# Neighbourhood projections as 512-wide products on four PSUM banks, five gates written beside the first attention, last key factors on the vector engine

## The chip, the cores and the metric

One core of a Trainium2 chip. The metric is the device time of one launch in microseconds (us); three executions of the kernel before took 1293.41, 1294.27 and 1298.26 us, so its median is 1294.27 us.

## What is computed

Two layers over 256 context and 256 latent tokens of width 1024, all in float32. Cut to what matters:

```
for l in range(2):
    mod = silu(c) @ w_ada[l] + b_ada[l]               # six rows of 1024: shift, scale, gate, twice
    p = modulate(rms_norm(x), sh1, sc1) @ w_in[l]     # one projection, by columns:
    gate_logits, c_q, c_kv, k_r, na = split(p)        # 2048 | 768 | 256 | 32 | 3 x 512
    mq = rms_norm(c_q) @ w_uq                         # 8 heads of 96
    k_nope, mv = rms_norm(c_kv) @ w_ukv               # 8 heads of 64 + 64
    mq, mk = rms_norm(mq), rms_norm(cat(k_nope, k_r)) # rotary part turned for latent tokens
    y_mla = softmax(mq mk') mv                        # the first attention
    nq, nk = rms_norm(na[0]), rms_norm(na[1]); nv = na[2]
    y_na = softmax(nq nk' + bias in a window, context keys) nv   # the second attention
    y = sigmoid(gate_a) * (y_mla @ w_mla_o) + sigmoid(gate_b) * (y_na @ w_na_o)
    x = x + gt1 * (y @ w_out)
    x = x + gt2 * (relu(modulate(rms_norm(x), sh2, sc2) @ w_ff1)^2 @ w_ff2)
```

Layer 1 is the last: queries, gates and all behind them are made there for the 256 latent tokens alone. Its modulation is computed during layer 0.

## The kernel before, in words

**Products.** Every projection is three TensorE products per block (`mm3`, lines 100 to 103): high by high, high by low, low by high. A weight tile of 1024 columns per partition comes from DRAM into one of 5 `raw` tiles (line 106); `wsplit` (lines 127 to 132) makes its high part on ScalarE (L130) and its low part on VectorE (L131) into one of 3 `whi`/`wlo` pairs. `proj_a` (lines 134 to 151) keeps the weights stationary; `proj_b` (line 561) keeps the tokens stationary and streams the weights, for two token blocks of 128 at a time.

**Order of the work.** A planner places the instructions: each engine takes the ready instruction that was written first, in a modelled clock, and the resulting order of each engine is fixed when the kernel runs. What is written later fills the time in which what is written earlier waits. Tiles of one name are handed out in the order in which they are written. The order around the change, within a layer, is:

1. query products with `w_uq` (lines 721 to 730): three column chunks of 288, 288 and 192; then `w_ukv` (lines 733 to 746), two chunks of 512;
2. statistics (`q_stat`, `k_stat`), key factors (`k_fin`, line 748) and the rotary part (`q_fin`, line 706), all on GpSimd (POOL);
3. `gates(NG0[l], "B")` (line 760): 6 of the 16 gate column blocks in layer 0, 8 in layer 1, in PSUM tiles `psB`. A gate is one weight tile and 24 products, 512 wide in layer 0 and 256 in layer 1; its tanh (L679) goes to DRAM. Then `step(99)` (line 761), the rest of the running modulation;
4. the first attention (`attend_mla`);
5. the neighbourhood projections (`chunk_na`, line 964): parts 1 (keys), 0 (queries), 2 (values), each as two halves of 256 columns, both token blocks of a pair in one `psA` tile; each half holds two weight tiles until its last token block is done;
6. the second attention (`attend_na`), whose bias additions (L816) are queued on POOL behind the last `q_fin` (line 815);
7. `gates(16 - ngate[0])` (line 1010): the other 10 gates of layer 0, 8 of layer 1, in `psA`; then `step(99)` (line 1011);
8. the merge: products with `w_mla_o` and `w_na_o`, and so on.

**Modulation beside it.** `ada_side` (line 236) is a generator that computes modulation rows on VectorE in steps; `step(n)` advances it by n. A row takes 8 steps of one weight tile each (two VectorE products of 128x1024, L251 for the first tile, L255 for the others; each queued on VectorE behind the latest `wlo` then written), two steps that transpose and sum the accumulators (L266, L267, through `tmp` tiles, which a gate's tanh uses too) and one that ends it with a product on TensorE (L273) and the bias (L277). In layer 0 row 2 runs up to the first attention. Rows 4 and 3, scale and shift of the second norm, follow from line 991 on; both use one accumulator tile named `v`, of which there is one, so row 3 starts when the sums of row 4 are done. Of their 22 steps 6 are taken in the neighbourhood projections and one per gate in item 7; `step(99)` writes what is left.

Of the kernel before, what the change touches and what calls it, by code (L numbers as in the profile page):

```python
# [14 lines left out]
KD = 8  # L15
# [30 lines left out]
def trunk(ctx: ExitStack, tc, t):  # L46
# [10 lines left out]
    def ps(tag):  # L57
        return pp.tile([128, 512], F32, tag="ps" + tag, name="ps" + tag, bufs=BANKS[tag])
# [406 lines left out]
    for l in range(DEPTH):  # L465
# [92 lines left out]

        turn = [0]

        def proj_b(load, nk, act_h, act_l, toks, N, evac, banks=None):

            tiles = [load(i) for i in range(nk)]
            total = sum(len(x[2]) for x in tiles)
            for p0 in range(0, len(toks), 2):
                pair = toks[p0:p0 + 2]
                if banks == "one":
                    o = ps("A")
                    outs = [o[:, i * N:(i + 1) * N] for i in range(2)]
                else:  # L570
                    turn[0] += 1
                    outs = [ps(b)[:, :N] for b in (banks[p0 // 2] if banks else ("AA", "BB")[turn[0] % 2])]
                parts = [list(zip(outs, pair))] if banks != "one" else [[x] for x in zip(outs, pair)]
                for part in parts:
                    n = 0
                    for wh, wl, ks in tiles:
                        for j, k in enumerate(ks):
                            for o, tk in part:
                                cs = slice(tk * 128, (tk + 1) * 128)
                                mm3(o, act_h(k)[:, cs], act_l(k)[:, cs], wh[:, j], wl[:, j], n == 0, n == total - 1)  # L580
                            n += 1
                for o, tk in zip(outs, pair):
                    evac(tk, o)

# [129 lines left out]
        def k_stat(t):  # L714
            z = krr[:, t:t + 2, :]
            nc.gpsimd.tensor_tensor(out=z, in0=z, in1=krs[:, t:t + 2].unsqueeze(2).to_broadcast([128, 2, NH]), op=ALU.add)
            fin_r(z.rearrange("p t h -> p (t h)"), z.rearrange("p t h -> p (t h)"), QK)
            nc.gpsimd.tensor_tensor(out=krz[:, t:t + 2, :], in0=z,
                                    in1=rk[:, t:t + 2].unsqueeze(2).to_broadcast([128, 2, NH]), op=ALU.mult)

        for h0, n in ((0, 3), (3, 3), (6, 2)):
            def evac(tk, o):
                dst = mq[:, tk, h0:h0 + n, :]
                nc.scalar.activation(out=dst, in_=o.rearrange("p (h d) -> p h d", h=n), func=AF.Copy)
                head_ss(qrs[:, tk, h0:h0 + n], dst, n, QK, rq[:, tk - q0:tk - q0 + 1])
                if h0 == 6 and tk % 2:
                    q_stat(tk - 1)

            proj_b(loader(t["w_uq"][l], 0, h0 * QK, n * QK, 3, 2), 2, lambda k: ch[:, k], lambda k: cl[:, k],
                   list(range(q0, 4)), n * QK, evac)  # L730


        for hf in range(2):
            def evac(tk, o):
                hs = slice(hf * 4, (hf + 1) * 4)
                src = o.rearrange("p (h d) -> p h d", h=4)
                rs = rk[:, tk:tk + 1]
                dst = mk[:, tk, hs, 0:NOPE]
                nc.vector.tensor_copy(dst, src[:, :, 0:NOPE])
                nc.scalar.activation(out=mv[:, tk, hs, :], in_=src[:, :, NOPE:128], func=AF.Copy, scale=rs)  # L740
                head_ss(krr[:, tk, hs], dst, 4, NOPE, rs)
                if hf == 1 and tk % 2:
                    k_stat(tk - 1)

            proj_b(loader(t["w_ukv"][l], 0, hf * 512, 512, 2, 1), 1, lambda k: ch[:, 6 + k], lambda k: cl[:, 6 + k],
                   [0, 1, 2, 3], 512, evac)

        def k_fin(tk):
            z = mk[:, tk, :, 0:NOPE]
            nc.gpsimd.tensor_tensor(out=z, in0=z, in1=krz[:, tk, :].unsqueeze(2).to_broadcast([128, NH, NOPE]),  # L750
                                    op=ALU.mult)
            nc.gpsimd.tensor_tensor(out=mk[:, tk, :, NOPE:QK], in0=kr[:, tk, :].unsqueeze(1).to_broadcast([128, NH, RD]),
                                    in1=krr[:, tk, :].unsqueeze(2).to_broadcast([128, NH, RD]), op=ALU.mult)

        for tk in range(4):
            k_fin(tk)
        for tk in range(q0, 4):
            q_end = q_fin(tk)

        gates(NG0[l], "B")  # L760
        step(99)


# [31 lines left out]
        def prep_na(hp):  # L795
# [165 lines left out]

        nrs = ap.tile([128, 8, NH], F32, name="nrs")

        def chunk_na(part, half, toks):
            def evac(tk, o):
                cs = slice(half * 256, (half + 1) * 256)
                if part == 2:
                    nc.scalar.activation(out=nv[:, tk, cs], in_=o, func=AF.Copy)
                    return
                i = 4 * part + tk  # L970
                nc.scalar.activation(out=nqk[:, i, cs], in_=o, func=AF.Copy)
                head_ss(nrs[:, i, half * 4:half * 4 + 4], nqk[:, i, cs].rearrange("p (h d) -> p h d", h=4), 4, HD)
                if half == 1:
                    fin_r(nrs[:, i, :], nrs[:, i, :], HD)
                    z = nqk[:, i, :].rearrange("p (h d) -> p h d", h=NH)
                    nc.gpsimd.tensor_tensor(out=z, in0=z, in1=nrs[:, i, :].unsqueeze(2).to_broadcast([128, NH, HD]),
                                            op=ALU.mult)

            proj_b(loader(w_in, 0, OFF_NA + part * 512 + half * 256, 256, 4, 8), 2, H, Lo, toks, 256, evac, "one")
# [341 lines left out]
```

## Time and profile before

| | |
|---|---|
| median of three executions | 1294.27 us |
| the profiled execution, its own time | 1295.01 us |
| its span, first to last instruction | 1293.2 us |
| TensorE (PE) busy | 1267.5 us, 98% |
| VectorE (DVE) busy | 913.5 us, 71% |
| ScalarE (ACT), GpSimd (POOL) busy | 582.5 and 264.2 us |
| mean granted TensorE clock | 0.997 of full speed |

A matmul's row lasts from its start to its modelled end and overlaps the next; how fast TensorE works is read from the distance between two starts. The busy share of an engine is the union of its rows, so a PE that is busy may still wait for less than a row's length between two products.

### The profile page before, as it was taken

Reading aid. Unit: us, or ns where it says so; the run is one execution under the profiler, and the core shown is the slowest. Engines: PE = TensorE matmul, PEld = TensorE weight load, DVE = VectorE, ACT = ScalarE, POOL = GpSimd, SP = SyncE. Lnnn points to the kernel's source line nnn. Section 1 sums busy time; section 2 is a strip of 40 time slices with the busy share of each in tenths; the row PEclk is TensorE's granted clock in tenths of the full one; section 3 lists DMA queues with packets and bytes.
Section 4 is the critical chain, followed back from the end, with each engine's and each line's share of the span. In section 5 each row is a group of like instructions: output and inputs, shape, how many; then the busy total and the mean of one; then the engine's idle time right before and its main releaser. Section 6 shows DMA issues by size and latency. Waiting matters only on the chain.

```text
span 1293.2 us, 20347 instructions
## 1 busy us (share of the span) xinstructions
PE 1267.5 (98%) x7831; PEld 1090.8 (84%) x7831; DVE 913.5 (71%) x1547; ACT 582.5 (45%) x1054; POOL 264.2 (20%) x258
## 2 busy tenths in 40 slices
PE   7999999999999999999999999999999999999997
PEld 5698878986788898888788888998889789999896
DVE  4557987588985579898897844766763977665553
ACT  4455376445523343422322312466664555555452
POOL 0317501411005003210210200019122112211011
PEclk9999999999999999999999999999999999999999
DMA  8854710364497316565598732487214658646652
GB/s 280 298 122 139 236 34 17 104 191 65 100 316 227 96 58 201 164 200 182 166 293 271 211 98 87 132 175 213 67 44 116 134 184 223 175 161 189 190 192 84
DMA packets 241730, 208.01 MB, mean 161 GB/s; under 512 B 24337, under 2 KB 220689, under 8 KB 241249
## 3 DMA queue, kind: packets, MB, share of 16 engines
q1 hardware_dynamic: 236112, 199.59, 53.1%
q10 hardware_dynamic: 5008, 6.85, 1.5%
q8 instruction: 61, 1.00, 0.3%
q0 software_dynamic: 512, 0.27, 0.1%
q14 instruction: 37, 0.30, 0.1%
HBM read 195.15 MB, written 11.53 MB: 160 GB/s over the span
## 4 chain that ended last, share of the span: by engine, by line
PE 52%; DVE 3%; DMA 2%; issue 2%; ACT 2%; POOL 2%; SPq 0%; POOLq 0%; ACTq 0%; DVEq 0%
PE psA L101 6%; PE psA L103 6%; PE psA L102 6%; PE psB L101 6%; PE psB L102 6%; PE psB L103 6%; PE psC L103 4%; PE psC L101 4%; PE psC L102 4%; ACT whi L130 1%; PE psC L871 1%; DVE wlo L131 1%; PE psD L891 1%; DMA raw<-in_w_out_dram 1%; DMA raw<-in_w_ukv_dram 1%
## 5 line engine op out<-in xcount | busy, mean ns | idle before, releaser
L131 DVE TENSOR_TENSOR wlo<-raw,whi 128x1024 fp32r<-128x1024 f32 (+3 forms) x252 | 312.3, 1240 | 174.6 <-ACT whi L130 171.3
L130 ACT ACTIVATE whi<-raw 128x1024 fp32r<-128x1024 f32 (+3 forms) x252 | 261.0, 1036 | 357.9 <-PE psB L102 104.3
L255 DVE SCALAR_TENSOR_TENSOR ada<-raw,silu,ada 128x1024 f32<-128x1024 f32 (+1 forms) x126 | 160.6, 1309 | 0.5
L101 PE MATMUL psA<-whi,h 128*128 128x256 f32 (+2 forms) x408 | 120.4, 295 | 0.5 <-ACT h L345 0.4
L103 PE MATMUL psA<-whi,h 128*128 128x256 f32 (+2 forms) x408 | 120.4, 295 | 0.0
L102 PE MATMUL psA<-wlo,h 128*128 128x256 f32 (+2 forms) x408 | 120.3, 295 | 0.0
L102 PE MATMUL psB<-h,whi 128*128 128x256 f32 (+1 forms) x272 | 91.9, 338 | 0.9 <-DVE h L1045 0.9
L101 PE MATMUL psB<-h,whi 128*128 128x256 f32 (+1 forms) x272 | 91.8, 338 | 0.0
L103 PE MATMUL psB<-h,wlo 128*128 128x256 f32 (+1 forms) x272 | 91.7, 337 | 0.0
L101 PE MATMUL psA<-h,whi 128*128 128x512 f32 (+1 forms) x248 | 87.7, 354 | 1.0 <-ACT h L345 0.8
L102 PE MATMUL psA<-h,whi 128*128 128x512 f32 (+1 forms) x248 | 87.4, 352 | 0.2 <-DVE h L347 0.2
L103 PE MATMUL psA<-h,wlo 128*128 128x512 f32 (+1 forms) x248 | 87.2, 352 | 0.0
L101 PEld LDWEIGHTS psA<-whi,h 128*128 128x128 f32 x408 | 77.9, 191 | 2.8 <-ACT h L345 0.9
L102 PEld LDWEIGHTS psA<-wlo,h 128*128 128x128 f32 x408 | 77.8, 191 | 2.5 <-issue 0.8
L103 PEld LDWEIGHTS psA<-whi,h 128*128 128x128 f32 x408 | 77.8, 191 | 1.9
L1174 POOL TENSOR_TENSOR h<-s,h 128x512 fp32r<-128x512 f32 (+1 forms) x32 | 38.7, 1210 | 170.7 <-ACT h L1173 153.3
L1174 POOL TENSOR_TENSOR fl<-s,fa 128x512 fp32r<-128x512 f32 (+1 forms) x32 | 35.1, 1098 | 163.9 <-ACT fa L1173 163.9
L101 PE MATMUL psB<-G,whi 128*128 128x512 f32 (+2 forms) x192 | 66.7, 347 | 0.0
L103 PE MATMUL psB<-G,wlo 128*128 128x512 f32 (+2 forms) x192 | 66.2, 345 | 0.3 <-DVE wlo L131 0.3
L102 PE MATMUL psB<-G,whi 128*128 128x512 f32 (+2 forms) x192 | 66.4, 346 | 0.0
L101 PE MATMUL psC<-G,whi 128*128 128x258 f32 (+2 forms) x200 | 62.7, 314 | 0.0
L102 PE MATMUL psC<-G,whi 128*128 128x258 f32 (+2 forms) x200 | 62.5, 312 | 0.0
(388 smaller groups left out, 3333.1 us busy)
## 6 DMA issues: line engine op xcount, KB each, us to landing
raw<-in_w_ff_dram SPq DMA_DIRECT2D x128, 512.0 KB, 4.1
raw<-in_w_ada_dram SPq DMA_DIRECT2D x80, 512.0 KB, 4.5
raw<-in_w_in_dram SPq DMA_DIRECT2D x62, 512.0 KB, 4.4
raw<-in_w_out_dram SPq DMA_DIRECT2D x16, 512.0 KB, 7.0
spare<-in_w_ada_dram SPq DMA_DIRECT2D x12, 512.0 KB, 8.9
xT_d<-xT SPq DMA_DIRECT2D x2, 2048.0 KB, 13.0
bias<-in_rpb_dram SPq DMA_DIRECT2D x64, 64.0 KB, 7.3
g_d<-g ACTq DMA_DIRECT2D x16, 256.0 KB, 4.5
```

The costliest lines, as they stand in the source:

```text
L101: nc.tensor.matmul(out, sh, mh, start=first, stop=False)
L102: nc.tensor.matmul(out, sh, ml, start=False, stop=False)
L103: nc.tensor.matmul(out, sl, mh, start=False, stop=last)
L130: first = nc.scalar.activation(out=hi, in_=src, func=AF.Copy).ins
L131: split[:] = [nc.vector.tensor_tensor(out=lo, in0=src, in1=hi.bitcast(F32), op=ALU.subtract).ins, first]
L255: nc.vector.scalar_tensor_tensor(out=a, in0=raw[:, c:c + w], scalar=sc, in1=a, op0=ALU.mult, op1=ALU.add)
L871: nc.tensor.transpose(o[:, kt * 256 + i * 128:kt * 256 + (i + 1) * 128], pt[:, (kp * 2 + kt) * 128:(kp * 2 + kt + 1) * 128], perm if K == ...
L891: mm = nc.tensor.matmul(yo[z * 64:(z + 1) * 64, oc], vsel(kt, 2 * hp + z), tr[kt // 2][:, kt % 2, :], start=kt == nkt - 1, stop=kt == 0, t ...
L1174: nc.gpsimd.tensor_tensor(out=al[:, f, :], in0=s[:, :TQ], in1=ah[:, f, :].bitcast(F32), op=ALU.subtract)
```

## The change

It does four things. The neighbourhood projections are 512 wide: a part is one product of 512 columns for all its token blocks at once, in four PSUM banks (two `psA`, and two `psB` or one `psD` and one `psB`), one weight tile after the other; in layer 1 the order of the parts is 0, 1, 2. The query product has two chunks of 512 and 256 columns and a modulation step behind each. The gates are 5 before the first attention, 5 written behind it and ahead of the start of rows 4 and 3, so that no step goes with these, and the other 6 beside the second attention, in both layers. In layer 1 `k_fin` of the two latent token blocks runs on VectorE; and the bias additions are queued on POOL behind the last `k_stat` rather than the last `q_fin`. The steps beside the projections are two behind part 0 and one per weight tile of part 2.

```diff
-NG0 = (6, 8)
+NG = ((5, 5), (5, 5))
...
-        for h0, n in ((0, 3), (3, 3), (6, 2)):
+        for c0, n, h0, nh, kper in ((0, 512, 0, 5, 2), (512, 256, 5, 3, 3)):
             def evac(tk, o):
...
+            proj_b(loader(t["w_uq"][l], 0, c0, n, kper, 6 // kper), 6 // kper, lambda k: ch[:, k], lambda k: cl[:, k],
+                   list(range(q0, 4)), n, evac)
+            step()
...
         def k_fin(tk):
             z = mk[:, tk, :, 0:NOPE]
+            eng = nc.vector if last and tk >= 2 else nc.gpsimd
...
-        gates(NG0[l], "B")
+        gates(NG[l][0], "B")
         step(99)
...
-                with tc.issue_after(q_end.ins):
+                with tc.issue_after(k_end[-1]):
...
-        def chunk_na(part, half, toks):
+        def chunk_na(part, toks, banks):
+
+            outs = [ps(b) for b in banks[:len(toks)]]
+            load = loader(w_in, 0, OFF_NA + part * 512, 512, 2, 4)
+            for i in range(4):
+                wh, wl, ks = load(i)
+                for j, k in enumerate(ks):
+                    for o, tk in zip(outs, toks):
+                        cs = slice(tk * 128, (tk + 1) * 128)
+                        mm3(o, hh[:, k, cs], hl[:, k, cs], wh[:, j], wl[:, j], k == 0, k == KD - 1)
+                if part == 2:
+                    step()
...
-            if (part, half) in ((0, 1), (2, 0), (2, 1)):
+            if part == 0:
                 step(2)
 
+        gates(NG[l][1])
         if l == 0:
             av = []
...
-        for part in (1, 0, 2):
-            for half in range(2):
-                chunk_na(part, half, list(range(q0, 4)) if part == 0 else [0, 1, 2, 3])
+
+        for part, banks in ((0, "AA"), (1, "AABB"), (2, "AADB")) if last else ((1, "AABB"), (0, "AABB"), (2, "AADB")):
+            chunk_na(part, list(range(q0, 4)) if part == 0 else [0, 1, 2, 3], banks)
```

## Rows read from the trace of the kernel before

**Rows 1.** The page: busy time of the engines.
```profile
PE 1267.5 (98%) x7831; PEld 1090.8 (84%) x7831; DVE 913.5 (71%) x1547; ACT 582.5 (45%) x1054; POOL 264.2 (20%) x258
```

**Rows 2.** Busy time by stretch. First the stretch in us, then its length, then busy us (instructions) of PE, PEld, DVE, ACT and POOL, the granted clock, the DMA share and GB/s. Layer 0: projections alone, second attention, the gates that are left; layer 1: projections alone, second attention.
```profile
234.00:276.00 42.00, 42.00 (x351) 42.00 (x352) 26.55 (x29) 16.70 (x32) 14.96 (x12) 1.00 0.51 154
276.00:352.00 76.00, 75.05 (x455) 51.81 (x454) 69.56 (x160) 43.16 (x105) 6.37 (x5) 1.00 0.47 96
352.00:376.00 24.00, 24.00 (x106) 19.84 (x107) 23.05 (x23) 6.89 (x9) 0.00 (x0) 1.00 0.83 261
...
964.00:1000.00 36.00, 36.00 (x303) 36.00 (x302) 11.42 (x15) 15.14 (x29) 12.53 (x13) 1.00 0.42 118
1000.00:1051.00 51.00, 50.63 (x375) 39.70 (x373) 47.05 (x96) 30.95 (x68) 5.56 (x4) 1.00 0.55 122
```

**Rows 3.** The timeline of PE at four places where nothing waits: start in us, length, engine, line, operation. Two pairs of starts in the query product (288 columns, five products from the first to the second; 192 columns, six), one in layer 0's gates up to the merge (512 columns, three) and one in layer 1's (256 columns, fifteen).
```profile
91.03 0.29 PE L101 MATMUL psB<-whi,G 128*128 128x288 f32 x1
...
91.69 0.30 PE L103 MATMUL psB<-whi,G 128*128 128x288 f32 x1
...
104.03 0.27 PE L101 MATMUL psA<-whi,G 128*128 128x192 f32 x1
...
104.70 0.28 PE L101 MATMUL psA<-whi,G 128*128 128x192 f32 x1
...
375.40 0.39 PE L101 MATMUL psA<-h,whi 128*128 128x512 f32 x1
...
376.08 0.39 PE L101 MATMUL psB<-ym,whi 128*128 128x512 f32 x1
...
1051.36 0.28 PE L101 MATMUL psA<-h,whi 128*128 128x256 f32 x1
...
1053.16 0.28 PE L101 MATMUL psB<-ym,whi 128*128 128x256 f32 x1
```

**Rows 4.** Busy PE time and number of the products into `psA` alone, which are what fills the two attentions (projections in the first, gates in the second). Layer 0: first attention, second attention, the rest up to the merge; layer 1: first and second attention, the rest up to the merge. Columns: stretch, length, busy us (products), clock, DMA share, GB/s.
```profile
157.00:232.00 75.00, 29.98 (x181) 0.98 0.12 37
275.60:352.00 76.40, 38.00 (x137) 1.00 0.47 97
352.00:376.10 24.10, 24.10 (x106) 1.00 0.83 261
909.30:963.70 54.40, 27.07 (x182) 1.00 0.14 42
999.60:1051.20 51.60, 26.01 (x179) 1.00 0.55 121
1051.20:1053.20 2.00, 2.00 (x16) 1.00 0.57 180
```

**Rows 5.** The timeline of DVE from layer 0's second attention to its merge: the rows of the weight splits (L131) and of the modulation (L251, L255, L266, L267) that the text uses.
```profile
275.43 1.23 DVE L131 TENSOR_TENSOR wlo<-raw,whi 128x1024 fp32r<-128x1024 f32 x1 [1.69 <-ACT whi L130]
276.57 1.28 DVE L255 SCALAR_TENSOR_TENSOR ada<-raw,silu,ada 128x1024 f32<-128x1024 f32 x1
...
279.09 1.28 DVE L255 SCALAR_TENSOR_TENSOR ada<-raw,silu,ada 128x1024 f32<-128x1024 f32 x1
280.29 1.22 DVE L131 TENSOR_TENSOR wlo<-raw,whi 128x1024 fp32r<-128x1024 f32 x1
...
337.83 0.70 DVE L266 STREAM_TRANSPOSE ada<-ada 128x512 f32<-128x512 f32 x1
...
343.27 0.67 DVE L267 TENSOR_REDUCE red<-ada 128x16 f32<-128x512 f32 x1
...
344.32 0.74 DVE L251 TENSOR_SCALAR ada<-raw,silu 128x1024 f32<-128x1024 f32 x1
...
346.71 1.22 DVE L131 TENSOR_TENSOR wlo<-raw,whi 128x1024 fp32r<-128x1024 f32 x1
...
361.97 9.65 DVE L255 SCALAR_TENSOR_TENSOR ada<-raw,silu,ada 128x1024 f32<-128x1024 f32 x8
371.54 2.35 DVE L131 TENSOR_TENSOR wlo<-raw,whi 128x1024 fp32r<-128x1024 f32 x2
```

**Rows 6.** The timeline of ACT in the same stretch: the tanh of the fourth of the ten gates, and the high part of the first merge weight.
```profile
334.52 0.59 ACT L679 ACTIVATE g<-psA 128x512 f32<-128x512 f32 x1
...
368.02 1.06 ACT L130 ACTIVATE whi<-raw 128x1024 fp32r<-128x1024 f32 x1 [2.02 <-DMA raw<-in_w_mla_o_dram]
```

**Rows 7.** The SP queue there: the issue of the first merge weight's load; and the landing times of the weight loads (L118) from 340 to 385 us.
```profile
362.08 0.38 SPq L118 DMA_DIRECT2D raw<-in_w_mla_o_dram  x1
...
DMA to landing us min/median/max: 4.1/5.1/6.2
```

**Rows 8.** The timeline of PE: the first transposes of layer 0's second attention, those of layer 1's, and the last products of layer 1's.
```profile
275.58 0.38 PE L799 MATMUL psC<-ident,nqk 128*128 128x128 f32 x2
...
999.66 0.38 PE L799 MATMUL psC<-rev,nqk 128*128 128x128 f32 x2
...
1050.61 0.60 PE L891 MATMUL psD<-PT,yv 128*64 128x256 f32 x4
```

**Rows 9.** Layer 1 ahead of the first attention: the first three bias additions and the last key factor on POOL, and the transpose on PE that waited for it.
```profile
881.58 4.82 POOL L816 TENSOR_TENSOR bias<-bias,wmask 128x512 f32<-128x512 f32 x3
...
908.65 0.61 POOL L752 TENSOR_TENSOR mqk<-kr,krr 128x256 f32<-128x256 f32 x1
...
909.32 0.32 PE L785 MATMUL psC<-ident,mqk 128*96 128x128 f32 x1 [0.34 <-POOL mqk L752]
```

More of the change, by code (lines that the diff above doesn't have):

```diff
@@ L559, in trunk, with proj_b @@
         turn = [0]
-        def proj_b(load, nk, act_h, act_l, toks, N, evac, banks=None):
+        def proj_b(load, nk, act_h, act_l, toks, N, evac):
             tiles = [load(i) for i in range(nk)]
@@ L566, in proj_b @@
                 pair = toks[p0:p0 + 2]
[L567 to L581, printed above, removed]
+                turn[0] += 1
+                outs = [ps(b)[:, :N] for b in ("AA", "BB")[turn[0] % 2]]
+                n = 0
+                for wh, wl, ks in tiles:
+                    for j, k in enumerate(ks):
+                        for o, tk in zip(outs, pair):
+                            cs = slice(tk * 128, (tk + 1) * 128)
+                            mm3(o, act_h(k)[:, cs], act_l(k)[:, cs], wh[:, j], wl[:, j], n == 0, n == total - 1)
+                        n += 1
                 for o, tk in zip(outs, pair):
@@ L717, in k_stat @@
             fin_r(z.rearrange("p t h -> p (t h)"), z.rearrange("p t h -> p (t h)"), QK)
-            nc.gpsimd.tensor_tensor(out=krz[:, t:t + 2, :], in0=z,
+            return nc.gpsimd.tensor_tensor(out=krz[:, t:t + 2, :], in0=z,
                                     in1=rk[:, t:t + 2].unsqueeze(2).to_broadcast([128, 2, NH]), op=ALU.mult)
-        for h0, n in ((0, 3), (3, 3), (6, 2)):
+        for c0, n, h0, nh, kper in ((0, 512, 0, 5, 2), (512, 256, 5, 3, 3)):
             def evac(tk, o):
[L723 to L726, printed above, removed]
+                flat = mq[:, tk].rearrange("p h d -> p (h d)")
+                nc.scalar.activation(out=flat[:, c0:c0 + n], in_=o, func=AF.Copy)
+                head_ss(qrs[:, tk, h0:h0 + nh], mq[:, tk, h0:h0 + nh, :], nh, QK, rq[:, tk - q0:tk - q0 + 1])
+                if c0 and tk % 2:
                     q_stat(tk - 1)
-            proj_b(loader(t["w_uq"][l], 0, h0 * QK, n * QK, 3, 2), 2, lambda k: ch[:, k], lambda k: cl[:, k],
-                   list(range(q0, 4)), n * QK, evac)
+            proj_b(loader(t["w_uq"][l], 0, c0, n, kper, 6 // kper), 6 // kper, lambda k: ch[:, k], lambda k: cl[:, k],
+                   list(range(q0, 4)), n, evac)
+            step()
+        k_end = []
         for hf in range(2):
@@ L742, in evac @@
                 if hf == 1 and tk % 2:
-                    k_stat(tk - 1)
+                    k_end.append(k_stat(tk - 1).ins)
             proj_b(loader(t["w_ukv"][l], 0, hf * 512, 512, 2, 1), 1, lambda k: ch[:, 6 + k], lambda k: cl[:, 6 + k],
@@ L962, in trunk @@
         nrs = ap.tile([128, 8, NH], F32, name="nrs")
-        def chunk_na(part, half, toks):
-            def evac(tk, o):
-                cs = slice(half * 256, (half + 1) * 256)
-                if part == 2:
-                    nc.scalar.activation(out=nv[:, tk, cs], in_=o, func=AF.Copy)
-                    return
-                i = 4 * part + tk
[L971 to L979, printed above, removed]
-            if (part, half) in ((0, 1), (2, 0), (2, 1)):
+        def chunk_na(part, toks, banks):
[3 more added lines that the diff above has]
+                wh, wl, ks = load(i)
+                for j, k in enumerate(ks):
+                    for o, tk in zip(outs, toks):
+                        cs = slice(tk * 128, (tk + 1) * 128)
+                        mm3(o, hh[:, k, cs], hl[:, k, cs], wh[:, j], wl[:, j], k == 0, k == KD - 1)
+                if part == 2:
+                    step()
+            for o, tk in zip(outs, toks):
+                if part == 2:
+                    nc.scalar.activation(out=nv[:, tk], in_=o, func=AF.Copy)
+                    continue
+                i = 4 * part + tk
+                z = nqk[:, i, :].rearrange("p (h d) -> p h d", h=NH)
+                nc.scalar.activation(out=nqk[:, i], in_=o, func=AF.Copy)
+                head_ss(nrs[:, i, :], z, NH, HD)
+                fin_r(nrs[:, i, :], nrs[:, i, :], HD)
+                nc.gpsimd.tensor_tensor(out=z, in0=z, in1=nrs[:, i, :].unsqueeze(2).to_broadcast([128, NH, HD]),
+                                        op=ALU.mult)
+            if part == 0:
                 step(2)
+        gates(NG[l][1])
         if l == 0:
```

6 lines of the change are left out of this document (3 added, 3 removed).

## The prediction

> **What bounds the kernel.** I read the page first: TensorE is busy for 98% of the span, every other engine for 71% or less [rows 1]. So time goes only where TensorE has less to do, or comes only where it runs dry. Then the table by stretch: outside the two attentions PE is busy for every microsecond at a granted clock of 1.00, 2.4 GHz, while VectorE has room (26.6 of 42 us beside layer 0's projections). Beside layer 0's second attention VectorE is busy for 69.6 of 76 us and for 23.1 of the 24 us behind it [rows 2]. That is the one place where a second engine is nearly full. Third, the distances between starts of products give TensorE's real pace [rows 3]. Last, the products into `psA` show how much filling each attention uses and how much is left when it ends [rows 4].
>
> **The change, part by part.**
>
> *Wide products.* Five products of 288 columns start over 0.66 us, six of 192 over 0.67, three of 512 over 0.68, fifteen of 256 over 1.80 [rows 3]: 0.132, 0.112, 0.227 and 0.120 us each. The projections have 24 products for each token block and half; with 3 parts of 4 blocks in layer 0 and 2 + 4 + 4 blocks in layer 1 that is 22 x 2 x 24 = 1056 products of 256, which become 528 of 512. Each pair gains 2 x 0.120 - 0.227 = 0.013 us: 6.9 us. The query product goes from 2 x 0.132 + 0.112 = 0.376 to 0.227 + 0.120 = 0.347 us for each of 6 x 3 x 6 = 108 places: 3.1 us. All of this lies on TensorE, so 10.0 us is the gain if nothing runs dry. The narrow rows say that a product costs about 13 ns beyond its columns, and that halving the count saves this. The Trainium skill, TensorE: Matmul & The Clock Gate, section Back-to-back issue gap, gives N / 2.4 GHz + 2.5 ns, hence 2.5 ns for each product saved; by that the two gains would be 1.6 us and not 10.0. The rows have both widths measured, so the sum goes by them.
>
> *First attention.* Of the 27 us (5 x 24 x 0.227) of gates now behind it and of the projections, layer 0's first attention needs about 181 x 0.120 = 22 us as filling, layer 1's likewise [rows 4]; the projections that it used to take are then made behind it, in PE time that is counted already. The tiles of `psB` and `psD` are handed out in written order, so a four-bank part can only begin its `psA` half beside this attention; the gates cover that. Nothing on the path: zero, between a loss of 2 us (the attention outlasts the gates) and a gain of 1.
>
> *Key factors and bias.* In layer 1 the four bias additions (4.82 us for the first three) leave their place ahead of the statistics on POOL, and two of the four blocks of key factors go to VectorE. The first transposes waited 0.34 us for the last factor [rows 9] and the gates covered the rest. They come up to 10 us earlier, but with 5 gates ahead of them in place of 8 (3 x 24 x 0.120 = 8.6 us less cover), and the next 5 gates stand by. Worth 0.3 us at most: zero. The four additions now wait behind the last `k_stat` and are used in the second attention, some 90 us later.
>
> *Other edits at zero.* The step behind each query chunk brings two VectorE steps and two weight loads on SP forward; `raw` tiles are left over, since the query product has 5 weight tiles in place of 6. The 512-wide evacuations, up to four in a row, run beside the next part, for which a third `psB` is free; if they don't, a part's border costs about one of 0.6 us, five times: 0 to 3 us.
>
> *Second attention, layer 0.* This is the price. Until now 10 gates stood behind this attention: 134 of their 240 products filled it and 106 ran alone in the 24 us behind it [rows 4]. In that time VectorE finished modulation row 3, eight products in one go, and only then, at 371.54, split the first two merge weights, though the high part of the first had been started at 368.02 [rows 5, 6]: row 3 is written earlier and goes first. TensorE began the merge at 376.08, with no wait [rows 3]. Now 6 gates stand there, with the same 6 steps before them. So row 4's last sum still comes behind the tanh of gate 4 (334.52, transposes from 337.83), and row 3, which needs the same accumulator, still begins only after that sum (343.27, then 344.32) [rows 5, 6]. From the attention's start at 275.58 [rows 8] row 3 starts 68.7 us in. From there to the end of the first merge split (371.54 + 1.2) were 28.4 us, of which four gates' splits at 1.22, 4.9 us, go: 23.5. The split is ready 92.2 us in. TensorE's work from the start to the merge was 376.08 - 275.58 = 100.5 us; four gates less (96 x 0.227 = 21.8) make it 78.7. TensorE would stand for 13.5 us. Against it, VectorE is relieved at the attention's start: the two splits and the two products at 275.43 to 280.29 [rows 5], 5.0 us, now come in the longer run of projections before it. As this stretch is bound by VectorE I count the relief in full: a stand of 8.5 us, with 13.5 above it and 0 below (if the merge splits get ahead of row 3).
>
> *Second attention, layer 1.* No modulation here. The 8 gates filled it all but exactly: 16 products were left, 2 us [rows 4]. From 999.66 to the merge at 1053.16 TensorE had 53.5 us of work [rows 3, 8]; two gates less (48 x 0.120 = 5.8) leave 47.7. The attention itself ended 51.5 us in (1050.61 + 0.60) [rows 8], VectorE being busy for 47 of 51 us [rows 2]: a stand of up to 3.8 us. Two gates' splits less, 2 x 1.22, shorten it by 2.4 if counted in full: 1.4 us, between 0 and 3.8.
>
> **Sum.** -6.9 - 3.1 + 8.5 + 1.4 = -0.1 us against the profiled execution's own 1295.0 us, which is 0.7 above the median of the three runs; on the median: **1294.2 us**. Half a per cent, 6.5 us, is about what a measurement of this kernel can tell from no change.
>
> **The rivals.**
>
> *The stands don't come (faster).* The planner gets row 3 done sooner, since the run of projections ahead of the second attention grows from 42 us [rows 2] to some 60 (12 token blocks x 24 x 0.227 = 65 us, a little of it earlier), and VectorE idles in a third of it; or it lets the merge splits pass. Then the 10.0 us stay: 1284.3, and up to 1287.8 with stands of 3.5 in all. For it: VectorE's total work up to the merge is not larger than before. Against it: the one accumulator and the order of the `tmp` tiles, seen at 334.52 to 344.32, don't allow an early start. Chance 0.35.
>
> *The merge weights come late (slower).* The place is the ring of 5 `raw` tiles. Row 3 takes eight of them, written ahead of the merge weights; in the trace the first merge weight's load was issued at 362.08, as VectorE began its last eight products of row 3 [rows 5, 7]. If it now gets a tile only when the last of these is done, landing (5.1 us median [rows 7]) and high part (1.06 us) come on top of the 13.5: 19.7 us, with 3.8 in layer 1 in all -10.0 + 23.5 = +13.5, 1307.8 us. It decides from stands of 16.5 us together. For it: the first five tiles are all taken by row 3 once the gates' loads are out. Against it: a tile comes free after every second product. Chance 0.13.
>
> *A product costs its columns and little more (slower).* In this kernel's terms: the 13 ns would belong to the place and not to the product, and the widths gain 1.6 us; with my stands 1302.6. The Trainium skill's formula above would have it so. Both widths run densely here with the distances given, so the trace speaks against it: chance 0.03.
>
> *It does not act as written.* The planner places gates and projections as before, whatever the order in the text, and only the widths count: this is the first rival's number and lies in its chance.
>
> **How the numbers follow.** The forecast, stands between 3.5 and 16.5 us, has 0.49; faster 0.35; slower 0.13 + 0.03 = 0.16. The range reaches from the faster rival's 1284.3, less 0.8 for what the first attention may give, 1283.5, to both stands at their upper ends, -10.0 + 17.3 = +7.3: 1301.6. Outside remain most of the slower rivals and a little below, under 0.2.
>
> **What would show it.** Right: neighbourhood products of 512 at 0.227 us in both layers; between layer 0's last attention product and the first of `w_mla_o` a gap on PE of about 8 us in which VectorE runs row 3 (L255) without a break and the wait on PE names `wlo`; about 1 us in layer 1. Wrong: no such gap, with row 3 done before the attention's end (first rival); a gap that ends with a load or `whi` (second); distances of 0.24 us (third). If the first attention shows new gaps before `psB` products, my zero there was wrong.

## The result and the profile after

The changed kernel takes 1308.91 us (median of 4 runs, 1307.02 to 1309.23) against 1295.13 us before, whose fourth execution, 1296.00, came with this measurement: a ratio of 1.0103, 95% interval 1.0088 to 1.0117. It is slower by 13.8 us where the forecast was 1294.2 and its range ended at 1301.6. The profiled execution took 1309.11 us with a span of 1307.3, 14.1 more than the one before.

The page of the changed kernel, busy time by engine, as [rows 1]: TensorE has fewer instructions and 96% in place of 98%.

```profile
PE 1261.2 (96%) x7195; PEld 1054.0 (81%) x7195; DVE 921.3 (70%) x1529; ACT 577.7 (44%) x1004; POOL 262.3 (20%) x254
```

**Where the time went.** For every product I took the distance from its start to the next start, and summed what lies beyond the dense distance of its shape (0.227 us for 512 columns, 0.120 for 256, and so on). The dense distances alone add up to 1198.5 us before and 1188.3 after: 10.2 less. The level of these sums hangs on what is taken as dense for the attentions' small products; with the median distance of each shape the differences between the two kernels, here and in the table, come out within 0.6 us of these. What is lost beyond them, in us by stage:

| stage | before | after |
|---|---|---|
| up to layer 0's first attention | 18.5 | 18.2 |
| layer 0, first attention and projections | 18.1 | 13.3 |
| layer 0, second attention | 16.9 | 17.6 |
| layer 0, merge | 0.1 | 15.8 |
| from there through layer 1's first attention | 19.2 | 29.9 |
| layer 1, second attention to the end | 14.7 | 16.9 |

So -10.2 (widths) -4.8 +0.7 +15.7 +10.7 +2.2 -0.3 makes 14.0 of the 14.1. The waits of PE, in total, times and longest, have the two large ones on top; neither is in before's trace at this size.

```profile
PE psB L103 <- DVE wlo L131: 10.2, 3, 9.5
PE psB L101 <- ACT whi L130: 8.5, 3, 6.9
...
PE psC L273 <- DVE red L267: 2.7, 1, 2.7
```

**The pace**, PE's timeline in layer 1's projections and in the query product. Eleven distances between products of 512 columns lie between 1014.63 and 1017.12 (0.226 each), and twelve of 256 between 102.73 and 104.17 (0.120), as [rows 3] had it for these widths elsewhere.

```profile
102.73 0.28 PE L103 MATMUL psA<-whi,G 128*128 128x256 f32 x1
...
104.17 0.28 PE L103 MATMUL psA<-whi,G 128*128 128x256 f32 x1
...
1014.63 0.39 PE L101 MATMUL psA<-whi,h 128*128 128x512 f32 x1
...
1017.12 0.39 PE L103 MATMUL psB<-whi,h 128*128 128x512 f32 x1
```

**Busy time by stretch**, columns as in [rows 2]: layer 0's projections alone, the second attention, the gates left, then three stretches of the stand at the merge.

```profile
225.00:286.00 61.00, 61.00 (x270) 50.48 (x270) 39.78 (x35) 23.40 (x31) 33.06 (x24) 1.00 0.50 150
286.00:352.00 66.00, 64.18 (x395) 43.77 (x393) 56.53 (x138) 40.59 (x99) 6.43 (x5) 1.00 0.38 69
352.00:366.00 14.00, 14.00 (x77) 10.73 (x76) 13.82 (x24) 2.40 (x4) 0.00 (x0) 1.00 0.46 151
366.00:373.00 7.00, 0.30 (x3) 0.00 (x0) 7.00 (x7) 1.47 (x2) 0.00 (x0) 0.68 0.78 254
373.00:383.00 10.00, 5.52 (x11) 3.09 (x12) 10.00 (x13) 2.31 (x3) 0.00 (x0) 0.50 0.57 173
383.00:386.00 3.00, 3.00 (x9) 2.32 (x8) 2.90 (x7) 0.00 (x0) 0.00 (x0) 0.58 0.97 378
```

VectorE is busy for 33.7 of the 34 us from 352 to 386, TensorE is all but idle from 366 to 373, and the granted clock falls from 1.00 to 0.50. The same place instruction by instruction, from the timelines of PE, DVE, ACT and SP, as [rows 3], [rows 5], [rows 6] and [rows 7] showed it before:

```profile
365.85 0.39 PE L103 MATMUL psA<-h,wlo 128*128 128x512 f32 x1
...
373.24 0.80 PE L101 MATMUL psB<-ym,whi 128*128 128x512 f32 x1 [6.94 <-ACT whi L130]
...
382.00 0.69 PE L273 MATMUL psC<-red,m 128*128 128x64 f32 x2 [2.72 <-DVE red L267]
...
383.44 0.63 PE L103 MATMUL psB<-ym,wlo 128*128 128x512 f32 x1
383.87 0.63 PE L101 MATMUL psB<-ym,whi 128*128 128x512 f32 x1
```

```profile
357.35 1.41 DVE L251 TENSOR_SCALAR ada<-raw,silu 128x1024 f32<-128x1024 f32 x2
...
362.76 14.43 DVE L255 SCALAR_TENSOR_TENSOR ada<-raw,silu,ada 128x1024 f32<-128x1024 f32 x12
...
381.86 1.22 DVE L131 TENSOR_TENSOR wlo<-raw,whi 128x1024 fp32r<-128x1024 f32 x1
...
372.13 1.06 ACT L130 ACTIVATE whi<-raw 128x1024 fp32r<-128x1024 f32 x1 [5.26 <-DMA raw<-in_w_mla_o_dram]
...
352.42 13.18 SPq L118 DMA_DIRECT2D raw<-in_w_ada_dram  x4
367.66 0.38 SPq L118 DMA_DIRECT2D raw<-in_w_mla_o_dram  x1
```

The last gate product starts at 365.85. Row 3 begins on VectorE at 357.35, its last twelve products run to 377.2 and its sums to 381.9; only then comes the first split of a merge weight. Its load had waited behind four loads of row 3 too, so the high part came at 372.13. The waits are 6.94, 1.05, 0.47 and 2.72 us; the rest of the 15.8 us are products 0.43 us apart at the lower clock (383.44 to 383.87).

**Layer 1 ahead of the first attention**, the stretch of [rows 9], from the timelines of PE, DVE and POOL of the changed kernel:

```profile
897.88 0.28 PE L102 MATMUL psB<-h,whi 128*128 128x256 f32 x1
907.65 0.58 PE L103 MATMUL psB<-h,wlo 128*128 128x256 f32 x1 [9.48 <-DVE wlo L131]
...
892.13 0.41 DVE L600 TENSOR_REDUCE krr<-sq 128x4 f32<-128x256 f32 x1
900.05 0.42 DVE L750 TENSOR_TENSOR mqk<-kr,krr 128x256 f32<-128x256 f32 x1 [7.51 <-POOL krr L180]
900.58 3.40 DVE L748 TENSOR_TENSOR mqk<-mqk,krz 128x512 f32<-128x512 f32 x2
903.91 1.48 DVE L750 TENSOR_TENSOR mqk<-kr,krr 128x256 f32<-128x256 f32 x1
905.31 4.55 DVE L131 TENSOR_TENSOR wlo<-raw,whi 128x1024 fp32r<-128x1024 f32 x3
...
897.11 2.91 POOL L180 TENSOR_TENSOR krr<-krr,mhalf 128x16 f32<-128x16 f32 x1
...
900.51 6.00 POOL L814 TENSOR_TENSOR bias<-bias,wmask 128x512 f32<-128x512 f32 x4
```

The two blocks of key factors that moved to VectorE stand in its order ahead of the fourth gate's split. The first of them waits 7.51 us for GpSimd's second statistic; everything behind it waits as well, and TensorE, which has gate 4's high part and not its low part, stands for 9.48 us.

### The profile page after: what moved, and what is told of

It reads as the page before. It is cut to its first block, busy times and chain, and to the rows that moved or that the text cites. A ratio compares the mean times of both kernels' runs of the same rounds, so it can differ in the third digit from the quotient of the medians.

```text
span 1307.3 us, 18992 instructions
## 1 busy us (share of the span) xinstructions
PE 1261.2 (96%) x7195; PEld 1054.0 (81%) x7195; DVE 921.3 (70%) x1529; ACT 577.7 (44%) x1004; POOL 262.3 (20%) x254
## 5 line engine op out<-in xcount | busy, mean ns | idle before, releaser
L131 DVE TENSOR_TENSOR wlo<-raw,whi 128x1024 fp32r<-128x1024 f32 (+3 forms) x250 | 315.5, 1263 | 175.0 <-ACT whi L130 174.2
L255 DVE SCALAR_TENSOR_TENSOR ada<-raw,silu,ada 128x1024 f32<-128x1024 f32 (+1 forms) x126 | 161.6, 1316 | 0.6
L101 PE MATMUL psA<-h,whi 128*128 128x512 f32 (+1 forms) x280 | 98.1, 351 | 1.0 <-ACT h L345 0.8
L102 PE MATMUL psA<-h,whi 128*128 128x512 f32 (+1 forms) x280 | 98.6, 352 | 0.2 <-DVE h L347 0.2
L103 PE MATMUL psA<-h,wlo 128*128 128x512 f32 (+1 forms) x280 | 97.9, 350 | 0.4 <-DVE wlo L131 0.4
L103 PE MATMUL psB<-h,wlo 128*128 128x512 f32 (+1 forms) x240 | 82.6, 344 | 9.5 <-DVE wlo L131 9.5
L101 PE MATMUL psB<-h,whi 128*128 128x512 f32 (+1 forms) x240 | 82.6, 345 | 1.3 <-ACT h L1050 1.3
L102 PE MATMUL psB<-h,whi 128*128 128x512 f32 (+1 forms) x240 | 82.7, 344 | 1.1 <-DVE h L1051 1.1
L103 PE MATMUL psC<-G,wlo 128*128 128x258 f32 (+2 forms) x200 | 62.5, 312 | 0.0
L101 PEld LDWEIGHTS psA<-h,whi 128*128 128x128 f32 x280 | 52.9, 189 | 7.9 <-ACT h L345 1.6
L103 PEld LDWEIGHTS psA<-h,wlo 128*128 128x128 f32 x280 | 53.1, 190 | 7.5 <-issue 1.8
L102 PEld LDWEIGHTS psA<-h,whi 128*128 128x128 f32 x280 | 53.1, 190 | 6.6 <-DVE h L347 0.8
L103 PEld LDWEIGHTS psB<-h,wlo 128*128 128x128 f32 x240 | 46.3, 193 | 15.0 <-DVE wlo L131 9.7
L101 PE MATMUL psA<-whi,h 128*128 128x512 f32 (+1 forms) x152 | 57.6, 379 | 0.4 <-ACT h L345 0.4
```

The costliest lines, as they stand in the source:

```text
L101: nc.tensor.matmul(out, sh, mh, start=first, stop=False)
L102: nc.tensor.matmul(out, sh, ml, start=False, stop=False)
L103: nc.tensor.matmul(out, sl, mh, start=False, stop=last)
L131: split[:] = [nc.vector.tensor_tensor(out=lo, in0=src, in1=hi.bitcast(F32), op=ALU.subtract).ins, first]
L255: nc.vector.scalar_tensor_tensor(out=a, in0=raw[:, c:c + w], scalar=sc, in1=a, op0=ALU.mult, op1=ALU.add)
```

## The experiments

My theory after this reading (A): two separate stands, one behind row 3 in layer 0 and one behind the key factors in layer 1, on top of a gain of 10 us from the widths. All times are medians; ratios are against the kernel before on the same chip, with 95% intervals. The runs were made on several chips, on which the kernel before took 1293.58 to 1295.21 us, so differences between runs are good to about 1.5 us.

**e1_kpool.** The factors go back to GpSimd.

```diff
-            eng = nc.vector if last and tk >= 2 else nc.gpsimd
+            eng = nc.gpsimd
```

> The changed kernel, with all four blocks of layer 1's key factors on GpSimd again; nothing else differs. Theory A (the factors stand in VectorE's order ahead of the splits of gates 4 and 5, and wait there for GpSimd's statistics): the splits pass, the stand of 9.5 us before gate 4 goes, and with it the 256-wide products that ran 0.21 us apart behind it: 10 to 11 us less than the changed kernel, about 1298.5. Rival B (five gates in place of eight are too few to cover the statistics, whoever makes the factors): the stand moves to the first transposes of layer 1's first attention and 1305 or more stays. Rival C (the stand is covered elsewhere anyway): 1308.

1303.25 us, 1.0060 (1.0036 to 1.0084): 5.7 less than the changed kernel, half of what A wanted. The stand before gate 4 is gone, but GpSimd's last factor ends at 907.74, and behind five gates a transpose of the first attention waits 2.29 us for it. A and B each have a part. The timelines of POOL and PE of this run:

```profile
899.51 3.76 POOL L180 TENSOR_TENSOR krr<-krr,mhalf 128x16 f32<-128x16 f32 x1
...
907.13 0.61 POOL L750 TENSOR_TENSOR mqk<-kr,krr 128x256 f32<-128x256 f32 x1
...
907.80 0.31 PE L783 MATMUL psC<-ident,mqk 128*96 128x128 f32 x1 [2.29 <-POOL mqk L750]
```

**e2_klate.** The factors stay on VectorE, behind the fifth gate's split.

```diff
-        for tk in range(4):
+        for tk in range(2 if last else 4):
             k_fin(tk)
...
         gates(NG[l][0], "B")
+        if last:
+            with tc.issue_after(split[0]):
+                k_fin(2)
+                k_fin(3)
```

> The changed kernel, with the two blocks of key factors still on VectorE, but queued behind the split of the fifth gate; nothing else differs. Theory A (place in the order): gates 4 and 5 run without a stand to about 903.7 on the old scale, the factors end at about 905.3 as before, and the splits of gates 6 to 8 come behind them: a stand of 2 to 3 us stays, about 1301 to 1303. Rival (it is VectorE's time for the factors, or their end, and not the place): 1307 to 1309.

1304.82 us, 1.0076 (1.0057 to 1.0095): 4.1 less, between the two. Place is worth that much; the rest goes with the late end of the factors themselves (910.1 here), which were made beside the bias additions.

**b1_kvec.** The kernel before, with the same two blocks on VectorE, its eight gates and its early bias kept.

```diff
+            eng = nc.vector if last and tk >= 2 else nc.gpsimd
-            nc.gpsimd.tensor_tensor(out=z, in0=z, in1=krz[:, tk, :].unsqueeze(2).to_broadcast([128, NH, NOPE]),
+            eng.tensor_tensor(out=z, in0=z, in1=krz[:, tk, :].unsqueeze(2).to_broadcast([128, NH, NOPE]),
...
```

> The kernel before, with only the change of engine for two blocks of layer 1's key factors. Theory A (the wait for the statistics in VectorE's order blocks the gates' splits, whatever their number): GpSimd's second statistic ended at 905.08 here and gates 4 to 8 stand behind it: TensorE stands for 10 to 14 us, 1305 to 1309. Rival B (eight gates cover what five don't): 1294 to 1296.

1308.34 us, 1.0099 (1.0083 to 1.0115): this one edit alone costs the kernel before 13 us. A is shown and B refuted: the gates that stand behind the blocked instruction cover nothing. PE's and DVE's timelines:

```profile
905.54 0.58 PE L103 MATMUL psB<-h,wlo 128*128 128x256 f32 x1 [10.63 <-DVE wlo L131]
...
902.19 0.42 DVE L753 TENSOR_TENSOR mqk<-kr,krr 128x256 f32<-128x256 f32 x1 [11.49 <-POOL krr L180]
902.72 1.29 DVE L751 TENSOR_TENSOR mqk<-mqk,krz 128x512 f32<-128x512 f32 x2
```

**e9_k82.** Factors on GpSimd, and eight gates ahead of layer 1's first attention, two beside it.

```diff
-NG = ((5, 5), (5, 5))
+NG = ((5, 5), (8, 2))
...
+            eng = nc.gpsimd
```

> The changed kernel, with layer 1's key factors on GpSimd alone and eight gates ahead of layer 1's first attention in place of five (two beside it in place of five). Theory A, as the run with the factors on GpSimd left it (its last factor ended at 907.74 and the transposes waited for it at the end of five gates): three gates more, 8.6 us, cover the rest of the statistics, 4 us less than that run's 1303.3: 1299. Rival (two gates and the projections are too little beside the first attention): the attention stands, 1303 or more.

1302.24 us, 1.0056 (1.0043 to 1.0070): 1.0 less than e1_kpool where 4 were expected. The layer-1 part came as A said, as distances lost up to and through that attention are 19.7 us, as before (19.2), against 22.8 in e1_kpool; 1.6 us of it went to the second attention and the merge (18.5 after 16.9), 2 to the start of this profile.

**e6_norow3.** Row 3 is left out; a copy of row 4 stands in its place.

> The changed kernel without layer 0's modulation row 3: its 16 products, transposes and sums on VectorE and its 8 weight loads are left out and the row is a copy of row 4 (so the output is not the reference's). Theory A (the stand at layer 0's merge is row 3 ahead of the merge weights, both in VectorE's order and in the ring of raw tiles): the whole 15.7 us that the distances between products lose there go, 1293 to 1296. Rival (too few gates are left for VectorE's other work): VectorE still ends last and 3 to 6 us stay, 1297 to 1301.

1292.43 us, 0.9978 (0.9968 to 0.9989): 16.5 less than the changed kernel; 0.8 us is lost at the merge in place of 15.8. Row 3 is the whole of that stand.

**e3_wfirst.** The first three merge weights ahead of row 3's last steps.

```diff
         gates(16 - ngate[0])
...
+        for _ in range(NHL):
+            weights()
         step(99)
...
-        for _ in range(NHL):
-            weights()
```

> The changed kernel, with the loads and splits of the first three merge weights written ahead of the last steps of modulation row 3 (in both layers); nothing else differs. Theory A (the stand at layer 0's merge comes from the order: row 3 goes ahead of the merge weights in the ring of raw tiles and on VectorE): the merge begins where the last gate ends, and of the 15.7 us lost there 3 to 5 remain, because the gates' products that the merge reads back come only when row 3 has freed their room and seven banks cover about 19 us: 1296 to 1299. Rival (VectorE simply has too much work there, whatever its order): the stand moves behind row 3 and 1305 or more stays.

1306.93 us, 1.0095 (1.0078 to 1.0111): the rival's time, but not wholly its reason. The merge began with no wait, at 366.26, and 15.9 us were lost a little later: seven loads of row 3 now stood ahead of the fourth weight, and a small product of row 3 held TensorE's order. VectorE was not full all the while: the third weight's split, now ahead of row 3, stood 4.34 us for its high part, and row 3 ended that much later. So the loss moved; that no order avoids it is not shown (PE, DVE and SP timelines).

```profile
381.27 0.50 PE L101 MATMUL psA<-ym,whi 128*128 128x512 f32 x1 [3.90 <-ACT whi L130]
390.09 0.69 PE L273 MATMUL psC<-red,m 128*128 128x64 f32 x2 [8.10 <-DVE red L267]
...
367.32 1.23 DVE L131 TENSOR_TENSOR wlo<-raw,whi 128x1024 fp32r<-128x1024 f32 x1 [4.34 <-ACT whi L130]
...
352.67 21.02 SPq L118 DMA_DIRECT2D raw<-in_w_ada_dram  x7
```

**e4_gates44.** Four and four gates in layer 0, so eight behind the second attention.

```diff
-NG = ((5, 5), (5, 5))
+NG = ((4, 4), (5, 5))
```

> The changed kernel, with four and four gates around layer 0's first attention in place of five and five, so that eight stand behind the second attention in place of six; nothing else differs. Theory A (the gates behind the second attention are the cover of row 3, 24 products of 0.227 us each): 10.9 us more of TensorE's work lies between row 3's start and the merge; of the 15.7 us lost at the merge about 5 remain and the first attention still has enough (eight gates' 44 us beside it and ahead of it): 1297 to 1300. Rival (row 3 moves with the gates, since its steps follow the gates in the text): 1306 to 1309.

1305.02 us, 1.0081 (1.0067 to 1.0096): 3.9 less. The merge loses 7.1 us in place of 15.8, near the 5 that A said, but half of this gain is given back ahead of the first attention, where a gate's split is now 2.60 us late at 141.53.

**e11_row3late.** Row 3 beside the merge.

```diff
-            side.append(ada_side(((0, 4, (0, 1)), (0, 3, (0, 1))), acc_v))
+            side.append(ada_side(((0, 4, (0, 1)),), acc_v))
...
+            sh = po.tile([128, 4096], F32, tag="fl", name="ada", bufs=1)
+            side.append(ada_side(((0, 3, (0, 1)),), lambda z: [sh[:, z * D:(z + 1) * D]]))
```

> The changed kernel, with layer 0's modulation row 3 taken out of the second attention and made beside the merge and the first blocks of the attention's output product, with accumulators in a room of its own that is free until the feed-forward part; nothing else differs. Theory A (row 3 is late only because it waits for row 4's accumulator and then stands ahead of the merge; VectorE is busy for 26.7 of the 44 us from 376 to 420 in the kernel before, so 23 us more nearly fit in there): TensorE's 15.7 us at the merge go and 1 to 4 come back: 1294 to 1298. Rival (VectorE's work is what counts, wherever it stands): the merge loses 10 us or more in smaller pieces, 1303 or more.

1306.53 us, 1.0084 (1.0067 to 1.0102): the rival again. The merge is clean (0.8 us lost), and the stand reappears where the output product begins. Busy time by stretch of this run: VectorE is full for 20 us and the clock falls.

```profile
405.00:415.00 10.00, 6.04 (x25) 4.12 (x24) 10.00 (x9) 2.93 (x5) 5.21 (x3) 0.89 0.38 111
415.00:425.00 10.00, 5.51 (x12) 3.93 (x13) 10.00 (x15) 2.00 (x3) 0.00 (x0) 0.50 0.54 157
```

**e12_best and e13_best81.** e11_row3late with factors on GpSimd and gates (8, 2), then (8, 1), in layer 1.

> The changed kernel with both stands undone and its wide products and its gates beside layer 0's first attention kept: row 3 beside the merge, key factors on GpSimd, eight gates ahead of layer 1's first attention and two beside it. Theory A (two separate stands, each with its own cause, and a gain of 10 us from the widths): the parts add up to the changed kernel less 12 to 15 us for row 3 and less 8 to 9 for the key factors: 1284 to 1288. Rival (the stands return elsewhere once these are gone): 1292 or more, no better than the kernel before.

> As the run before, with one gate beside layer 1's first attention in place of two, so that seven stand behind its second attention. Theory A (the second attention's gates cover VectorE's work ahead of layer 1's merge, where the distances between products lose 4.4 us more than before): 1 to 2 us less than the run before. Rival (the first attention lacks the gate's 2.9 us as filling): 1 to 3 us more.

1296.20 us, 1.0013 (1.0001 to 1.0024), and 1295.13 us, 1.0001 (0.9989 to 1.0014): layer 1's stand adds its 10 us as a part of its own, and layer 0's stays. A's 1284 to 1288 was missed, since e11_row3late had moved layer 0's stand and not removed it. Undoing layer 1's stand was worth 6.7 us on the changed kernel (e9_k82), 10.3 here and 11.0 from e14_steps to e15_s1_81. One gate's difference is 1.1 us, within the spread of the runs.

**e14_steps.** Row 4 starts beside the first part of the projections, where VectorE is free (39.78 of 61 us busy from 225 to 286, and 7.96 of the first 25).

```diff
-                if part == 2:
+                if part == 2 or l == 0 and part == 1:
                     step()
```

> The changed kernel, with four more modulation steps, one behind each weight tile of the first projection part in layer 0; nothing else differs. Theory A (rows 4 and 3 begin too late: VectorE is busy for only 10.5 of 30 us from 220 to 250, ahead of row 4's first product at 251.28): four steps of two products at 1.2 us each, 10 us and the idle ahead of them, come out of the stretch that VectorE bounds; of the 15.7 us at the merge 1 to 5 remain: 1295 to 1298. Rival B (VectorE's work is too much wherever it stands, or the early products hold up the splits of the projections): 1304 or more.

1298.34 us, 1.0022 (1.0008 to 1.0037): 10.6 less than the changed kernel with nothing else touched; the merge loses 7.5 us in place of 15.8, the second attention 15.0 in place of 17.6. A, 0.3 us above its range.

**e15_s1_81 and e16_s3_81.** e14_steps with layer 1 undone as in e13_best81; then two steps more ahead of the attention. The line that sets the steps in the second, against the changed kernel:

```diff
-                if part == 2:
+                if part == 2 or l == 0 and (part == 0 or i >= 2):
                     step()
```

> The run before and, in layer 1, key factors on GpSimd alone with eight gates ahead of the first attention and one beside it. Theory A: both stands are gone and the widths' 10 us and layer 0's first attention (4.8 us less lost than before) are left: 1281 to 1286, faster than the kernel before and than the kernel before with the wide query product alone (1289.3). Rival B: 1291 or more.

> As the run before, with the steps spread otherwise: none behind the first two weight tiles of the first projection part, two behind its last two, and six in place of two in the second part, so that two steps more are made ahead of the second attention. Theory A (what counts is how much of rows 4 and 3 is done ahead of the attention): 0 to 2 us less than the run before. Rival (the second part's steps collide with its evacuations and its products into GpSimd): 2 to 4 us more.

1287.39 us, 0.9931 (0.9911 to 0.9952), and 1281.17 us, 0.9886 (0.9866 to 0.9906). The first is 1.4 us above A's range, the second gains 6.2 us on it where 0 to 2 were expected. The second beats the kernel before by 14 us, about what the widths (10.2) and layer 0's first attention (4.8) gave. Row 3 begins at 274.75 in it, ahead of the attention, and the merge loses 1.5 us. Its busy time by stretch, over the same stretches as above, and the row's first products on DVE:

```profile
225.00:286.00 61.00, 61.00 (x271) 50.48 (x271) 51.59 (x53) 23.18 (x31) 31.38 (x24) 1.00 0.62 181
...
366.00:373.00 7.00, 7.00 (x33) 5.80 (x32) 4.43 (x11) 1.06 (x1) 0.00 (x0) 1.00 0.66 243
373.00:383.00 10.00, 10.00 (x46) 8.27 (x45) 6.99 (x8) 3.40 (x4) 6.05 (x4) 1.00 0.85 335
...
274.75 1.41 DVE L251 TENSOR_SCALAR ada<-raw,silu 128x1024 f32<-128x1024 f32 x2
```

VectorE was busy for 11.8 us more beside the projections. So its work as a whole need not shrink: what helped was to take more of rows 4 and 3 out of the full stretch and into the earlier one. Row 3 begun at 357.35 (changed kernel), 284.18 (e14_steps) and 274.75 left 15.8, 7.5 and 1.5 us at the merge.

**b2_wuq.** The kernel before with the query product alone widened.

```diff
-        for h0, n in ((0, 3), (3, 3), (6, 2)):
+        for c0, n, h0, nh, kper in ((0, 512, 0, 5, 2), (512, 256, 5, 3, 3)):
...
```

> The kernel before, with only the query product in columns of 512 and 256 in place of 288, 288 and 192 (and the weight tiles that go with it). By the distances of 0.132, 0.112, 0.227 and 0.120 us: 108 times 0.029 us less, 1292.1. By the Trainium skill, TensorE: Matmul & The Clock Gate, section Back-to-back issue gap (N / 2.4 GHz + 2.5 ns): 108 times 0.0025 us, 1294.9.

1289.28 us, 0.9961 (0.9947 to 0.9974): 4.9 less, 3.4 to 6.9 by the interval. The dense distances fall by 3.1 (1198.5 to 1195.4), as the rows gave; in the profiles the rest came from less lost in and ahead of the first attentions (1.0 and 1.8 us). In layer 0 the same two waits stand in both profiles (1.33 and 0.51 us, here 1.35 and 0.51), but the clock fell behind them in the kernel before alone; in layer 1 a wait of 0.90 us for a ScalarE copy (`mv`, at 879.60) is gone. Why these went is not shown.

## Why the prediction was wrong

Against the forecast of -0.1 us stand 14.1. The key factors cost 10.7 more than forecast, layer 0's merge 7.2, the rest of the second attentions 1.5; layer 0's first attention and what lies ahead of it gave 5.1 back, the widths 0.2 more than forecast.

*Wide products: right.* 10.0 us were forecast and the dense distances fell by 10.2, 3.1 of it in the query product. The Trainium skill's formula (TensorE: Matmul & The Clock Gate, section Back-to-back issue gap), which that section calls the gap of a product by itself, would have 1.6 and 0.3; the trace disagrees with it for these products.

*Key factors and bias: this step failed.* "Worth 0.3 us at most: zero" was 10.7 us. I asked who covers the wait (the gates) and not what is queued behind the instruction that waits: on VectorE that was the gates' own splits, so the cover was stopped by what it was to cover. b1_kvec shows it alone, at 13 us. The rows were nearly at hand: beside the last factor at 908.65 and the transpose that waited for it [rows 9], the kernel before's timeline of POOL has the second statistic's end at 904.79, while a gate's split stood in VectorE's order every 2.9 us by then (900.80, 903.68, 906.56).

```profile
901.02 3.77 POOL L180 TENSOR_TENSOR krr<-krr,mhalf 128x16 f32<-128x16 f32 x1
```

Two smaller parts came with it. Five gates do not cover GpSimd's chain (2.3 us in e1_kpool). And the bias additions, which I counted as harmless behind the last statistic, ran at the same moment as the factors: 3.40 us for two of L748 here, 1.29 for the same two in b1_kvec, where GpSimd was idle.

*Second attention, layer 0: the right mechanism, sized too small.* Row 3 did start late and did stand ahead of the splits: it began 70.8 us after the attention's start (357.35, the attention's first transposes being at 286.53; forecast 68.7), and the first low part was ready 96.6 us in (forecast 92.2). What failed is the term "I count the relief in full", 5.0 us: the two splits less at the attention's start brought row 3 no earlier. Row 4's last product had ended on VectorE at 286.26, yet its sums began only at 346.59, and the last two of its four transposes came behind the tanh of gate 4 at 351.40, 64.9 us in (58.9 before). So row 3's start went with the gates and not with VectorE's load at the attention's start; this fits the prediction's reading of the `tmp` tiles, which no run tests by itself. The timelines of PE, DVE and ACT of the changed kernel:

```profile
286.53 0.38 PE L797 MATMUL psC<-ident,nqk 128*128 128x128 f32 x2
...
346.59 0.69 DVE L266 STREAM_TRANSPOSE ada<-ada 128x512 f32<-128x512 f32 x1
...
351.40 0.60 ACT L673 ACTIVATE g<-psA 128x512 f32<-128x512 f32 x1
```

Without the relief the forecast's upper end, 13.5, stood. The measured 15.7 us are, by the profile's names, 11 us of waits and 4.6 of products at half clock, which I had not priced. What set the length was the first low part, ready at 383.08. From the end of the gates' work at 366.3 to the first product that needs a low part (383.44) lie some 17 us, in which TensorE ran ten products that need the high part alone, 2.3 us at full pace; about 1 us of half clock came behind. The first 6.94 us were a wait for a high part, the sign that the prediction gave its second rival, and the ring of `raw` tiles did let that load go only at 367.66. But an earlier load alone would have let those ten products run sooner and TensorE wait for the same low part (argued from these rows; no run moves the load alone). With layer 1's loss that rival had no part in, so its 1307.8 is near the result by luck: the sum behind it is another.

*Second attention, layer 1: the right number, by luck.* 2.2 us were lost more from there to the end, 1.4 forecast between 0 and 3.8. But the stand at the merge that was forecast did not come: the merge began at 1061.24, without a wait, while the attention still ran. The loss lies behind it, where the output product waits for its input `h`, twice where it was once before. PE's timeline of the changed kernel, then of the one before:

```profile
1092.03 0.39 PE L101 MATMUL psB<-h,whi 128*128 128x256 f32 x1 [1.30 <-ACT h L1050]
...
1093.92 0.38 PE L102 MATMUL psB<-h,whi 128*128 128x256 f32 x1 [1.14 <-DVE h L1051]
```

```profile
1079.89 0.39 PE L102 MATMUL psB<-h,whi 128*128 128x256 f32 x1 [0.90 <-DVE h L1045]
```

*First attention: zero forecast, 4.8 us gained in layer 0.* Before, no product of the projections stood there to fill in from 173.05 to 182.68, TensorE ran dry and the mean clock from 170 to 180 us was 0.83; with gates as filling neither happened. No run changes this filling by itself. The same ten microseconds of the kernel before, then of the changed one:

```profile
170.00:180.00 10.00, 8.16 (x56) 6.83 (x56) 7.32 (x13) 6.54 (x12) 0.00 (x0) 0.83 0.35 106
```

```profile
170.00:180.00 10.00, 10.00 (x63) 7.67 (x62) 7.70 (x21) 6.90 (x16) 0.00 (x0) 1.00 0.08 31
```

*The rivals.* "The stands don't come" needed row 3 sooner in the longer run of projections. The room was there (e16_s3_81 uses it), but the steps are written behind the second part, so row 4 began at 251.28 as the text has it. The planner did not do what the text did not ask.

## What to carry to other kernels

When an operation is moved to another engine, list what stands behind it in that engine's order and how long its input is late: cover that depends on the same queue is no cover. When filling is taken from behind a stage, the side work that ran in its shadow has to start earlier by as much; find the earlier stretch in which that engine idles, since putting it elsewhere in the full stretch (e3_wfirst, e11_row3late) only moved the stand here.

## What the runs showed of the hardware

The granted clock fell from 2.4 to 1.2 GHz in both stands of the changed kernel: its mean was 0.68 while TensorE stood from 366 to 373 at layer 0's merge and 0.50 in the ten microseconds behind, and it was low behind the 9.48 us in layer 1. Products of 512 columns then started 0.43 us apart, those of 256 0.22 (908.24 to 908.46), until the clock rose. By the distances that was 4.6 and about 1.6 us beside the waits; of the 4.6 only about 1 us lies behind 383.44, where TensorE no longer waited for VectorE.

VectorE and GpSimd slow each other on operations with two inputs in SBUF: VectorE's L748 took 1.70 us beside the bias additions, and the same operation 0.65 in b1_kvec with GpSimd idle; in e11_row3late three row products took 6.19 us beside GpSimd's work against 1.20 each in the changed kernel. In e1_kpool a split on VectorE took 2.08 us and GpSimd's L750 beside it 1.60, against 1.23 and 0.61 elsewhere in that run. The Trainium skill, SBUF — State Buffer, section SBUF: two separate sides, states that such an operation and one of GpSimd that reads SBUF exclude each other for a whole instruction; the longer times agree with that.
